# Attention loads reordered with the keys loaded once, and outputs scaled and stored by groups of blocks

## The chip, the cores and the metric

The kernel runs on one core of one Trainium2 chip. The metric is the device time of one execution in microseconds (us). Engines are named as in the profile: PE is TensorE (PEld its weight loads), DVE is VectorE, ACT is ScalarE, POOL is GpSimd, SP is SyncE, which here only issues transfers (DMAs). PEclk is the share of full speed that TensorE's clock was granted.

## What is computed

Two layers of a model over 2048 latent tokens (a grid of 32 rows by 64 columns) behind 256 context tokens, width 1024, all in float32. A layer is: modulation and layer norm, one input projection, three head groups side by side (A: 6 windowed heads on 2 key heads; B: a gated short convolution; C: 6 neighbourhood heads), an output projection, a residual norm, a mixture of 16 experts, a residual norm. The change is in the attention of A and C:

```python
# A: latent queries see a band of +-128 tokens, all context keys and a sink; context queries see the context and the sink
s_win = jnp.einsum('bnqkgd,bnjkd->bnkgqj', qb, kw).astype(jnp.float32) * scale
s_win = jnp.where(valid[None, :, None, None], s_win, NEG_INF)
s_ctx = jnp.einsum('bnqkgd,bjkd->bnkgqj', qb, k_ctx).astype(jnp.float32) * scale
p_win, p_ctx, _ = joint_softmax([s_win, s_ctx, s_sink])
o = (jnp.einsum('bnkgqj,bnjkd->bnqkgd', p_win.astype(v.dtype), vw)
     + jnp.einsum('bnkgqj,bjkd->bnqkgd', p_ctx.astype(v.dtype), v_ctx))
...
# C: a query sees 8 rows x 16 columns around it, with a bias by relative position (rpb), and all context keys
s_nb = s_nb + jnp.transpose(bias, (1, 0, 2, 3, 4))[None].astype(jnp.float32)
s_nb = jnp.where(col_ok[None, None, None, :, None, :], s_nb, NEG_INF)
p_nb, p_ctx = joint_softmax([s_nb, s_ctx])
```

## The kernel before

Every float32 operand of a matmul is split into a high and a low part, and products of parts are added in PSUM. A layer runs four phases one after the other: `phase_in` (projection), `phase_att`, `phase_out` (output projection), `phase_moe`. `phase_in` takes the tokens in five chunks of up to 512; the chunk's transposed input lies in the pool `hT` (two buffers of `hh` and `hl`, taken in turn) and its results (queries QA and QC, keys KA and KC, values VS, the convolution's OB) go to DRAM.

`phase_att` goes through *blocks* in the order of `blist`. A has two units (key heads) of 16 latent blocks and, in layer 0 alone, two context blocks, 36 or 32 blocks of three *members* (the three query heads of 128 tokens). C has six units (heads): in layer 0 a context block (n = 4, two members), and then four blocks (n = 0 to 3) of four members, one per column region. A member passes through `qk` (logits, L1042 and L1043), `soft_max` (bias or mask added, and the minimum, L1064 on DVE), `soft_exp` (L1072 on ACT), transposes on PE, a copy to high parts (L1201 on ACT) and the low parts (L1192 on DVE). When a block's members are through, `pv` multiplies by the values (L1147), copies the sum (L1153, ACT), transposes it (L1160), and then finishes the block: in A the sink's exponent (L1155 DVE, then ACT) and its addition (L1165 DVE); the reciprocal of the sums (L1167 DVE); the addition of high and low halves (L1163 ACT, L1169 DVE); the multiplication by the reciprocal (L1172 DVE); the store, one SP transfer in A (L1174) and for n = 4 (L1176), four in C (L1180; those of the very last block on POOL).

The order on each engine is the order of the program: the loop at L1207 goes through the members three stages apart by the strings ORDERA and ORDERC, and the generators of `pv` advance at "R". Engines wait on one another only by what they read and write.

Transfers. All loads go through SP's queue, in order. At the first member of a block `qk` calls `load_block` up to two blocks ahead (queries, L973 in A and L981 in C; in C also four transfers of the values `vw`, L986) and, at the fifth block of an A unit or the second of a C unit, `load_unit` for the next unit. `load_unit` fetches keys in four transfers of 64 partitions (L948): the high half twice, into partitions 0 to 63 and 64 to 127 of one tile, and the low half twice into another, since queries lie in 128 partitions as [high; low] and the products of both go in one matmul. It also fetches the values (`va` or `vx`) and, by 16 POOL transfers (L962), the table `toep` out of rpb; the very first keys come in two pieces, with maskA (L953) between. `bias_part` (L1004) forms a bias on POOL, three parts for a bias, into one of two buffers (`bias`, and a `va` tile that C no longer needs).

Memory is handed out by pools in order of opening; the first tile of a pool waits for all users of older tiles that lay under the pool. `phase_out` opens its pools over those of attention; the ring of weights (class W) splits raw weights by an ACT cast (L178, called in `_high`) and a DVE subtraction (L186), and its loads of the stored results are L1247 and L1258.

```python
V.tensor_tensor(o[:, :nm, :], o[:, :nm, :], rec["rs"][:, :nm, None].to_broadcast([128, nm, 64]), op=ALU.mult)
```

Of the kernel before, what the change touches and what calls it, by code (L numbers as in the profile page):

```python
# [21 lines left out]
TT = SEQ + CTX  # L22
# [202 lines left out]
def build(ctx, tc, t, out):  # L225
# [279 lines left out]
    def phase_in(l):  # L505
# [5 lines left out]
        hT = {}  # L511
# [102 lines left out]
        def gemm(c):  # L614
# [52 lines left out]
            def b_rest(what, j, pg):  # L667
# [41 lines left out]
                if what == "b":  # L709
# [13 lines left out]
                    for a, o in enumerate((oh, ol)):  # L723
                        for r0, r1, d in runs:
                            (G if c == 4 else SY).dma_start(OB[l][j, :, a, d + r0:d + r1], o.bitcast(F32)[:, r0:r1])
# [169 lines left out]
    def phase_att(l):  # L895
        es = ExitStack()
        kp = es.enter_context(tc.tile_pool(name="at_k", bufs=2))
        qp = es.enter_context(tc.tile_pool(name="at_q", bufs=3))
# [27 lines left out]
        NM = len(mem)  # L926
        ulist = [("A", u) for u in range(2)] + [("C", u) for u in range(6)]
        ustart = {x: min(j for j, b in enumerate(blist) if b[:2] == x) for x in ulist}

        def load_unit(kind, u):  # L930
            r = units[kind, u] = {}
            src = (KA if kind == "A" else KC)[l][u]
            ks = r["k"] = [kp.tile([128, TT], F32R, name=f"k{a}") for a in range(2)]
            vs = VS[l].rearrange("(i p) h d -> p i h d", p=128)
            if kind == "A":
                r["v"] = v = vp.tile([128, NT, 128], F32R, name="va")

            pieces = ((0, 5), (5, NT)) if not blks else ((0, NT),)
            first = not blks
            if first:  # L940
                load_block(blist[0])
            for t0, t1 in pieces:
                if first and t0:
                    for b in blist[1:3]:
                        load_block(b)
                for a in range(2):
                    for b in range(2):
                        SY.dma_start(ks[a].bitcast(F32)[64 * b:64 * b + 64, 128 * t0:128 * t1],  # L948
                                     src[a][:, 128 * t0:128 * t1])
                if t0 == 0 and len(pieces) > 1:  # L950
                    SY.dma_start(maskA, t["maskA"])
                if kind == "A":
                    SY.dma_start(v.bitcast(F32)[:, t0:t1], vs[:, t0:t1, u, :])  # L953
            if kind == "C":
# [3 lines left out]
                tz = bp.tile([128, 16, 48], F32, name="toep", bufs=2)  # L958
# [1006 lines left out]
```

## Time and profile before

| what | value |
|---|---|
| median of 3 runs | 4175.27 us (4169.72 to 4181.32) |
| the profiled execution's own time | 4169.93 us |
| its span | 4168.1 us, 64121 instructions |
| PE, PEld busy | 3816.9 us (92%), 3252.6 us (78%) |
| DVE, ACT, POOL busy | 2906.3 us (70%), 2007.4 us (48%), 826.0 us (20%) |
| transfers | 789.93 MB, mean 190 GB/s |
| attention of layer 0 | about 624 to 1070 us |
| attention of layer 1 | about 2734 to 3170 us |

The span is what the hardware profiler records of one execution. The two attentions are a fifth of it (446 and 436 us). Busy shares over the whole span mix stages with different limits, so the rows below are taken from stretches.

### The profile page before, as it was taken

How to read it: one execution, taken by the hardware profiler on the slowest of the kernel's cores; microseconds unless marked ns; L12 is line 12 of the kernel's file. 1: busy time of each engine (PE TensorE's matmuls, PEld its weight loads, DVE VectorE, ACT ScalarE, POOL GpSimd, SP SyncE). 2: the span in 40 equal slices, each digit the busy share in tenths (PEclk: the TensorE clock that was granted, in tenths of full speed). 3: DMA queues.
4: the chain of work that ended last, by engine and by line, in shares of the span. 5: the costliest groups of instructions: out<-in, count | busy, mean ns of one | idle time of the engine just before them, and what ended most of it. 6: DMA issues, size and time to landing. Idle time of an engine off the chain costs nothing. (4 is left out here: it accounts for less than half of the span.)

```text
span 4168.1 us, 64121 instructions
## 1 busy us (share of the span) xinstructions
PE 3816.9 (92%) x22980; PEld 3252.6 (78%) x22980; DVE 2906.3 (70%) x5836; ACT 2007.4 (48%) x3918; POOL 826.0 (20%) x850
## 2 busy tenths in 40 slices
PE   7999998999998899999997999989989975999983
PEld 5877777888787388989876888778887864999972
DVE  6555557999677477777747765479886776777765
ACT  4344337988433044444424433368775332444453
POOL 0000000144132023323311000011441220222214
PEclk9999998999998999999998999999999986999996
DMA  7566665388643777777766766663786433888885
GB/s 228 170 215 189 203 179 136 82 183 175 226 158 120 217 238 222 211 212 216 210 180 221 220 196 184 174 161 80 147 166 216 168 125 124 251 253 249 246 243 183
DMA packets 733942, 789.93 MB, mean 190 GB/s; under 512 B 121808, under 2 KB 612952, under 8 KB 729784
## 3 DMA queue, kind: packets, MB, share of 16 engines
q1 hardware_dynamic: 692392, 656.83, 54.1%
q0 software_dynamic: 41232, 129.01, 11.4%
q8 instruction: 182, 2.98, 0.3%
q14 instruction: 136, 1.11, 0.1%
HBM read 607.08 MB, written 178.48 MB: 188 GB/s over the span
## 5 line engine op out<-in xcount | busy, mean ns | idle before, releaser
L178 ACT CAST wh<-wraw 128x1024 fp32r<-128x1024 f32 x636 | 656.4, 1049 | 380.8 <-DMA wraw<-in_w_in 132.2
L186 DVE TENSOR_TENSOR wl<-wraw,wh 128x1024 fp32r<-128x1024 f32 x636 | 751.1, 1215 | 17.6 <-ACT wh L178 17.4
L1192 DVE TENSOR_TENSOR pl<-pt,ph 128x256 fp32r<-128x256 f32 (+2 forms) x792 | 359.9, 494 | 21.3 <-ACT ph L1201 16.8
L1201 ACT CAST ph<-pt 128x256 fp32r<-128x256 f32 (+2 forms) x792 | 309.1, 446 | 96.2 <-PE pt L1089 88.7
L626 PE MATMUL gem<-hh,wh 128*128 128x512 f32 (+1 forms) x960 | 355.1, 370 | 0.0
L627 PE MATMUL gem<-hl,wh 128*128 128x512 f32 (+1 forms) x960 | 353.1, 368 | 0.0
L1072 ACT ACTIVATE p<-lg,mx 128x640 f32<-128x640 f32 (+3 forms) x408 | 331.9, 813 | 40.1 <-DVE mx L1064 38.8
L628 PE MATMUL gem<-hh,wl 128*128 128x512 f32 (+1 forms) x960 | 350.6, 365 | 0.0
L1809 PE MATMUL pu<-xh,wh 128*128 128x288 f32 (+1 forms) x1024 | 304.1, 297 | 7.0 <-DVE sa L1637 7.0
L1809 PE MATMUL pa<-xh,wh 128*128 128x288 f32 (+1 forms) x1024 | 300.5, 293 | 0.7 <-DVE modc L419 0.7
L1811 PE MATMUL pa<-xh,wl 128*128 128x288 f32 (+1 forms) x1024 | 296.7, 290 | 0.8 <-DVE wl L186 0.8
L1811 PE MATMUL pu<-xh,wl 128*128 128x288 f32 (+1 forms) x1024 | 296.2, 289 | 0.0
L1810 PE MATMUL pa<-xl,wh 128*128 128x288 f32 (+1 forms) x1024 | 294.0, 287 | 0.0
L1810 PE MATMUL pu<-xl,wh 128*128 128x288 f32 (+1 forms) x1024 | 293.8, 287 | 0.0
L1548 POOL DMA_INDIRECT xe<-H,ix x80 | 161.7, 2021 | 476.3 <-DVE ix L1543 398.3
L1671 POOL DMA_INDIRECT ACC<-y,ix x62 | 128.8, 2077 | 579.6 <-DVE y L1652 326.9
L1846 PE MATMUL py<-wh,gh 128*128 128x512 f32 x512 | 206.4, 403 | 19.6 <-ACT gh L1639 10.8
L804 PE MATMUL gem<-wh,hh 128*128 128x512 f32 x544 | 221.0, 406 | 0.4 <-ACT hh L595 0.4
L805 PE MATMUL gem<-wl,hh 128*128 128x512 f32 x544 | 217.4, 400 | 1.4 <-DVE wl L186 1.4
L806 PE MATMUL gem<-wh,hl 128*128 128x512 f32 x544 | 217.3, 399 | 0.0
L626 PEld LDWEIGHTS gem<-hh,wh 128*128 128x128 f32 x960 | 182.7, 190 | 31.4
L628 PEld LDWEIGHTS gem<-hh,wl 128*128 128x128 f32 x960 | 182.7, 190 | 31.1
(352 smaller groups left out, 9975.1 us busy)
## 6 DMA issues: line engine op xcount, KB each, us to landing
wraw<-in_w_in SPq DMA_DIRECT2D x160, 512.0 KB
wraw<-in_w_gate SPq DMA_DIRECT2D x128, 512.0 KB
wraw<-in_w_up SPq DMA_DIRECT2D x128, 512.0 KB
wraw<-in_w_down SPq DMA_DIRECT2D x128, 512.0 KB
wraw<-in_w_mod SPq DMA_DIRECT2D x88, 512.0 KB
k<-KC SPq DMA_DIRECT2D x48, 576.0 KB
vw<-VS SPq DMA_DIRECT2D x192, 128.0 KB
VS<-vs SPq DMA_DIRECT2D x36, 512.0 KB
```

Source lines behind the costliest of these rows:

```text
L178: self.nc.scalar.copy(h, self.raw[i])
L186: self.nc.vector.tensor_tensor(e[1], self.raw[i], e[0].bitcast(F32), op=ALU.subtract)
L626: P.matmul(pg[:, t0:nt], wh[:, cs_], hh[:, k, t0:nt], start=(k == 0), stop=False)
L627: P.matmul(pg[:, t0:nt], wh[:, cs_], hl[:, k, t0:nt], start=False, stop=False)
L628: P.matmul(pg[:, t0:nt], wl[:, cs_], hh[:, k, t0:nt], start=False, stop=(k == KD - 1))
L804: P.matmul(pg, hh[:, k, tk], wh[:, cs_], start=(k == 0), stop=False)
L1072: S.activation(p[:, 0:768 - w0], rec["lg"][:, w0:768], AF.Exp, bias=st[b]["mx"][:, m:m + 1], scale=-1.0, accum_out=st[b]["ss"][:, m:m + 1])
L1192: V.tensor_tensor(view(st[b]["pl"]), src, view(st[b]["ph"].bitcast(F32)), op=ALU.subtract)
L1201: S.copy(view(st[b]["ph"]), src)
L1809: P.matmul(pp[f], wh[:, cs_], xh[:, kk, :], start=(kk == 0), stop=False)
L1810: P.matmul(pp[f], wh[:, cs_], xl[:, kk, :], start=False, stop=False)
L1811: P.matmul(pp[f], wl[:, cs_], xh[:, kk, :], start=False, stop=(kk == KD - 1))
```

## The change

- `hT` starts with a dummy pair of tiles, so that each chunk uses the other buffer than before. The OB stores of chunk 4 go through ACT's queue instead of POOL's.
- The pools of attention are opened in another order: keys, queries, `vw`, bias, maskA, values, and then the others; the output tiles (`at_o`) come near the end, three tiles of 12 members instead of six of four.
- Keys come as one tile [high; low] by one transfer of 128 partitions. Queries lie in four fixed tiles with two halves, [high; high] and [low; 0]; the zeros are written once per layer by POOL. A block's queries come by three transfers of 64 partitions, three blocks ahead; `vw` stays two ahead.
- `toep` comes by one SP transfer, in rows read backwards by `bias_part`.
- Blocks are put in groups (A: four blocks, or the two context blocks; C: two blocks, or one). Minima, sums, reciprocals and outputs of a group lie in one tile each; L1155, L1165, L1167 and L1172 are done once per group, L1172 on POOL (the last block's on DVE), and the group is stored then.

The diff, cut to its core (removed lines stand in the functions above):

```diff
         last = l == DEPTH - 1
-        hT = {}
+        hT = {-1: [hp.tile([128, KD, 512], F32R, name=z) for z in ("hh", "hl")]}
...
-                            (G if c == 4 else SY).dma_start(OB[l][j, :, a, d + r0:d + r1], o.bitcast(F32)[:, r0:r1])
+                            (S if c == 4 else SY).dma_start(OB[l][j, :, a, d + r0:d + r1], o.bitcast(F32)[:, r0:r1])
...
         kp = es.enter_context(tc.tile_pool(name="at_k", bufs=2))
-        qp = es.enter_context(tc.tile_pool(name="at_q", bufs=3))
+        qp = es.enter_context(tc.tile_pool(name="at_q", bufs=1))
+        vwp = es.enter_context(tc.tile_pool(name="at_vw", bufs=3))
+        bsp = es.enter_context(tc.tile_pool(name="at_bias", bufs=1))
+        mp = es.enter_context(tc.tile_pool(name="at_m", bufs=1))
+        vp = es.enter_context(tc.tile_pool(name="at_v", bufs=2))
         sm = es.enter_context(tc.tile_pool(name="at_s", bufs=4))
         pp = es.enter_context(tc.tile_pool(name="at_p", bufs=3))
         hp = es.enter_context(tc.tile_pool(name="at_h", bufs=2))
-        op = es.enter_context(tc.tile_pool(name="at_o", bufs=6))
         wp = es.enter_context(tc.tile_pool(name="at_w", bufs=2))
-        vp = es.enter_context(tc.tile_pool(name="at_v", bufs=2))
+        op = es.enter_context(tc.tile_pool(name="at_o", bufs=3))
...
-        maskA = bp.tile([128, 640 + 512], F32, name="maskA")
+        maskA = mp.tile([128, 640 + 512], F32, name="maskA")
         maskC = bp.tile([128, 3 * MWID], F32, name="maskC")
-        biases = [None, bp.tile([128, BWID], F32, name="bias")]
+        biases = [None, bsp.tile([128, BWID], F32, name="bias")]
...
+        group = {}
+        for kind, u in [("A", 0), ("A", 1)] + [("C", u) for u in range(6)]:
+            for rows in (range(2, 6), range(6, 10), range(10, 14), range(14, NT), (0, 1)) if kind == "A" else (
+                    ((4,), (0, 1), (2,), (3,)) if u == 5 else ((4,), (0, 1), (2, 3))):
+                for j, n in enumerate(rows):
+                    group[kind, u, n] = ((kind, u, rows[0]), j, len(rows))
...
+        qs = [qp.tile([128, 2, 4, 128], F32R, name=f"q{i}") for i in range(4)]
+        for q in qs:
+            G.memset(q.bitcast(F32)[64:128, 1], 0.0)
...
-            src = (KA if kind == "A" else KC)[l][u]
-            ks = r["k"] = [kp.tile([128, TT], F32R, name=f"k{a}") for a in range(2)]
+            src = (KA if kind == "A" else KC)[l][u].rearrange("a d n -> (a d) n")
+            k = r["k"] = kp.tile([128, TT], F32R, name="k")
             vs = VS[l].rearrange("(i p) h d -> p i h d", p=128)
+            first = loaded[0] == 0
             if kind == "A":
...
+            for t0, t1 in ((0, 5), (5, NT)) if first else ((0, NT),):
+                if first:
+                    more_queries(1 if t0 == 0 else 4)
+                SY.dma_start(k.bitcast(F32)[:, 128 * t0:128 * t1], src[:, 128 * t0:128 * t1])
+                if first and t0 == 0:
                     SY.dma_start(maskA, t["maskA"])
...
-                tz = bp.tile([128, 16, 48], F32, name="toep", bufs=2)
+                tz = bp.tile([128, 16, 64], F32, name="toep", bufs=2)
                 rp = t["rpb"][l, u]
-                tv = tz.rearrange("(a b) i j -> a b i j", a=8)
-                for b in range(16):
-                    G.dma_start(tv[:, b], bass.AP(tensor=rp.tensor, offset=rp.offset + 15 * 64 + 15 - b,
-                                                   ap=[[64, 8], [-64, 16], [1, 48]]))
+                n = 15 * 64 + 48
+                SY.dma_start(tz.rearrange("p i j -> p (i j)")[:, 0:n],
+                             bass.AP(tensor=rp.tensor, offset=rp.offset + 15, ap=[[64, 8], [-1, 16], [1, n]]))
                 r["toep"] = tz
...
+            q = r["q"] = qs[at % 4]
+            for x, a, y in ((0, 0, 0), (0, 1, 0), (1, 0, 1)):
+                dst = q.bitcast(F32)[64 * a:64 * a + 64, x]
+                if kind == "A":
+                    SY.dma_start(dst[:, 0:3], QA[l][3 * u:3 * u + 3, y, :, 128 * n:128 * n + 128].rearrange("m d n -> d m n"))
+                    continue
+                src = QC[l][u][y]
+                if n == 4:
+                    SY.dma_start(dst[:, 0:2], src[:, 0:256].rearrange("p (m q) -> p m q", m=2))
+                else:
+                    SY.dma_start(dst.rearrange("p m (h q) -> p (m h) q", h=2),
+                                 src[:, 256:].rearrange("p (m g q) -> p m g q", m=8, g=4)[:, :, n, :])
...
+            blks[b]["vw"] = vw = vwp.tile([128, 8, 128], F32R, name="vw")
             vsr = VS[l][256:TT, 2 + u, :].rearrange("(r a c) d -> a c r d", a=4, c=64)
             for a in range(4):
                 SY.dma_start(vw.bitcast(F32)[32 * a:32 * a + 32], vsr[a, CG0[n]:CG0[n] + 32])
...
-                            tz[:, i0:i0 + n, j0:j0 + 32], op=ALU.subtract)
-        loaded = [0]
+                            bass.AP(tensor=tz.tensor, offset=tz[:, 15 - i0:16 - i0, j0:j0 + 32].offset,
+                                    ap=[tz.ap[0], [-64, n], [1, 32]]), op=ALU.subtract)
...
                 x = ulist.index((kind, u)) + 1
-                while loaded[0] < min(at + 3, len(blist)):
-                    load_block(blist[loaded[0]])
-                    loaded[0] += 1
+                more_queries(at + 4)
+                more_values(at + 3)
                 if at == ustart[kind, u] + (4 if kind == "A" else 1) and x < len(ulist):
                     load_unit(*ulist[x])
...
-            kh, kl = units[kind, u]["k"]
-            q = blks[b]["q"][:, m, :]
+            k = units[kind, u]["k"]
+            q = blks[b]["q"]
...
-            for x, k in enumerate((kh, kl)):
+            for x in range(2):
                 if win:
-                    P.matmul(pl[:, w0:512], q, win(k), start=(x == 0), stop=(x == 1))
-                P.matmul(pl[:, 512:768], q, k[:, 0:256], start=(x == 0), stop=(x == 1))
+                    P.matmul(pl[:, w0:512], q[:, x, m, :], win(k), start=(x == 0), stop=(x == 1))
+                P.matmul(pl[:, 512:768], q[:, x, m, :], k[:, 0:256], start=(x == 0), stop=(x == 1))
...
             if m == 0:
-                st[b] = {z: sm.tile([128, 4], F32, name=z) for z in ("mx", "ss", "rs")}
+                g, j, ng = group[b]
+                if j == 0:
+                    st["of", g] = {z: sm.tile([128, 12], F32, name=z)[:, 0:ng * nm] for z in ("mx", "ss", "rs")}
+                st[b] = {z: x[:, j * nm:j * nm + nm] for z, x in st["of", g].items()}
...
+            g, j, ng = group[b]
+            of = st["of", g]
+            end = j == ng - 1
+            if end and kind == "A":
+                V.tensor_tensor(of["rs"].rearrange("p (b m) -> p b m", b=ng),
+                                sink[:, None, 3 * u:3 * u + 3].to_broadcast([128, ng, 3]),
+                                of["mx"].rearrange("p (b m) -> p b m", b=ng), op=ALU.subtract)
+                S.activation(of["rs"], of["rs"], AF.Exp, scale=-1.0)
...
-            o = op.tile([128, 4, 64], F32, name="o")
-            S.copy(o[:, :nm, :], px[:, :nm, 64:128])
+            if j == 0:
+                of["o"] = op.tile([128, 12, 64], F32, name="o")[:, 0:ng * nm, :]
+            all_ = of["o"]
+            o = all_[:, j * nm:j * nm + nm, :]
+            S.copy(o, px[:, :nm, 64:128])
+            if end and kind == "A":
+                V.tensor_tensor(of["ss"], of["ss"], of["rs"], op=ALU.add)
+            yield
+            if end:
+                V.reciprocal(of["rs"], of["ss"])
+            yield
+            V.tensor_tensor(o, px[:, :nm, 0:64], o, op=ALU.add)
+            del st[b], blks[b]
+            if not end:
+                return
+            yield
+            yield
+            (V if b == blist[-1] else G).tensor_tensor(all_, all_, of["rs"][:, :, None].to_broadcast([128, ng * nm, 64]),
+                                                       op=ALU.mult)
+            n0 = g[2]
             if kind == "A":
-                V.tensor_tensor(rec["ss"][:, :nm], rec["ss"][:, :nm], rec["rs"][:, :nm], op=ALU.add)
...
-            if kind == "A":
-                SY.dma_start(MIXA[l][128 * n:128 * n + 128, 192 * u:192 * u + 192], o[:, 0:3, :].rearrange("p m d -> p (m d)"))
+                SY.dma_start(MIXA[l][128 * n0:128 * (n0 + ng), 192 * u:192 * u + 192].rearrange("(b p) c -> p b c", p=128),
+                             all_.rearrange("p (b m) d -> p b (m d)", b=ng))
...
+                for x in range(ng):
+                    for m in range(4):
+                        (G if b == blist[-1] else SY).dma_start(dst[m, n0 + x], all_[:, 4 * x + m, :])
+            del st["of", g]
```

## Rows read from the trace of the kernel before

**Rows 1.** Windows: stretch, length; busy us per engine (instructions); PEclk; DMA share; GB/s.

```profile
690.00:840.00 150.00, 147.02 (x1028) 132.30 (x1026) 147.70 (x465) 136.00 (x409) 16.54 (x25) 1.00 0.34 92
842.00:1066.00 224.00, 213.26 (x1548) 188.35 (x1548) 208.82 (x508) 188.82 (x478) 90.16 (x112) 1.00 0.83 176
2932.00:3164.00 232.00, 209.73 (x1479) 189.80 (x1477) 198.66 (x463) 178.30 (x438) 90.28 (x112) 0.95 0.76 161
```

**Rows 2.** Timeline of DVE, one A block: start, duration, instruction.

```profile
781.00 0.86 DVE L1064 CUSTOM_DVE_ANT_0 lg<-lg,maskA,sinks 128x640 f32<-128x640 f32 x1
...
783.65 0.35 DVE L1172 TENSOR_TENSOR o<-o,rs 128x192 f32<-128x192 f32 x1
783.92 0.15 DVE L1155 TENSOR_TENSOR rs<-sinks,mx 128x3 f32<-128x3 f32 x1
784.00 0.88 DVE L1192 TENSOR_TENSOR pl<-pt,ph 128x384 fp32r<-128x384 f32 x2
...
785.60 0.15 DVE L1165 TENSOR_TENSOR ss<-ss,rs 128x3 f32<-128x3 f32 x1
785.78 0.89 DVE L1192 TENSOR_TENSOR pl<-pt,ph 128x384 fp32r<-128x384 f32 x2
786.59 0.17 DVE L1167 RECIPROCAL rs<-ss 128x3 f32<-128x3 f32 x1
786.67 0.86 DVE L1064 CUSTOM_DVE_ANT_0 lg<-lg,maskA,sinks 128x640 f32<-128x640 f32 x1
```

**Rows 3.** First softmax of each layer on DVE (idle before), and SP’s wait.

```profile
631.64 0.76 DVE L1064 CUSTOM_DVE_ANT_0 lg<-lg,maskA,sinks 128x512 f32<-128x512 f32 x1 [10.09 <-PE lg L1043]
...
2740.90 0.76 DVE L1064 CUSTOM_DVE_ANT_0 lg<-lg,maskA,sinks 128x512 f32<-128x512 f32 x1 [9.84 <-DMA maskA<-in_maskA]
...
SPq L973 <- PE gem L628: 8.5, 1, 8.5
```

**Rows 4.** Windows, L1064 alone on DVE: length, busy (records), PEclk, DMA share, GB/s.

```profile
631.60:690.00 58.40, 22.96 (x50) 0.85 0.68 146
2740.90:2795.00 54.10, 22.96 (x50) 0.90 0.75 158
```

**Rows 5.** Waits of PE from 620 to 840: total us, times, longest.

```profile
PE lg L1042 <- DMA k<-KA: 13.0, 3, 4.5
```

**Rows 6.** Windows, C of layer 1: blocks 1 and 2; then 3 and 0.

```profile
2980.95:2997.50 16.55, 16.55 (x124) 15.06 (x124) 16.20 (x39) 14.64 (x37) 3.23 (x4) 1.00 0.62 144
2997.50:3020.45 22.95, 19.25 (x126) 17.65 (x125) 16.65 (x39) 14.96 (x37) 16.02 (x23) 0.85 0.98 184
```

**Rows 7.** Waits of PE from 2700 to 3200.

```profile
PE lg L1042 <- DMA qc<-QC: 17.4, 4, 4.8
```

**Rows 8.** Timeline of SP’s queue, one unit of C in layer 1.

```profile
2950.82 2.38 SPq L948 DMA_DIRECT2D k<-KC  x4
...
2954.39 0.43 SPq L981 DMA_DIRECT2D qc<-QC  x1
```

**Rows 9.** Windows: key loads of 64 partitions; then weights of 128 partitions.

```profile
2993.50:2999.50 6.00, 6.00 (x48) 5.66 (x47) 5.91 (x14) 5.09 (x12) 3.29 (x3) 1.00 1.03 222
3182.00:3198.00 16.00, 15.29 (x68) 11.88 (x67) 5.24 (x8) 2.95 (x5) 0.00 (x0) 1.00 0.92 332
```

**Rows 10.** Groups of DVE, 2932 to 3164: busy, mean ns of one, idle before.

```profile
L1172 DVE TENSOR_TENSOR o<-o,rs 128x256 f32<-128x256 f32 x22 | 20.8, 943 | 0.0
```

**Rows 11.** GpSimd’s bias parts: group of C, layer 0; then its queue’s waits (min/median/max ns).

```profile
L1004 POOL TENSOR_TENSOR bias<-maskC,toep 128x512 f32<-128x512 f32 x8 | 10.3, 1283 | 18.1 <-DVE mx L1064 18.1
...
L1004 POOLq EVENT_SEMAPHORE  x96: 17/30/10038, 746.7 to 3134.8; - x96
```

**Rows 12.** End of attention, layer 0: ACT’s first cast; SP’s wait, 1050 to 1080.

```profile
1070.82 1.99 ACT L178 CAST wh<-wraw 128x1024 fp32r<-128x1024 f32 x2
...
SPq L1247 <- DMA MIXC<-o: 2.7, 1, 2.7
```

More of the change, by code (lines that the diff above doesn't have):

```diff
@@ L964, in load_unit, with load_queries @@
+                SY.dma_start(tz.rearrange("p i j -> p (i j)")[:, 0:n],
+                             bass.AP(tensor=rp.tensor, offset=rp.offset + 15, ap=[[64, 8], [-1, 16], [1, n]]))
                 r["toep"] = tz
-        def load_block(b):
+        def load_queries(at):
+            b = blist[at]
             kind, u, n = b
-            if b in blks:
-                return
-            r = blks[b] = {}
-            if kind == "A":
-                r["q"] = qp.tile([128, 3, 128], F32R, name="qa")
-                SY.dma_start(r["q"].bitcast(F32), QA[l][3 * u:3 * u + 3, :, :, 128 * n:128 * n + 128].rearrange(
-                    "m a d n -> (a d) m n"))
-                return
-            r["q"] = q = qp.tile([128, 4, 128], F32R, name="qc")
-            src = QC[l][u].rearrange("a d n -> (a d) n")
-            if n == 4:
-                SY.dma_start(q.bitcast(F32)[:, 0:2], src[:, 0:256].rearrange("p (m q) -> p m q", m=2))
-                return
-            SY.dma_start(q.bitcast(F32).rearrange("p m (h q) -> p (m h) q", h=2),
-                         src[:, 256:].rearrange("p (m g q) -> p m g q", m=8, g=4)[:, :, n, :])
-            r["vw"] = vw = qp.tile([128, 8, 128], F32R, name="vw")
@@ new lines, in load_queries @@
+            r = blks[b] = {}
+            q = r["q"] = qs[at % 4]
[10 more added lines that the diff above has]
+                                 src[:, 256:].rearrange("p (m g q) -> p m g q", m=8, g=4)[:, :, n, :])
@@ L984, in load_block, with load_values @@
+        def load_values(at):
+            b = blist[at]
+            kind, u, n = b
+            if kind == "A" or n == 4:
+                return
+            blks[b]["vw"] = vw = vwp.tile([128, 8, 128], F32R, name="vw")
             vsr = VS[l][256:TT, 2 + u, :].rearrange("(r a c) d -> a c r d", a=4, c=64)
@@ L986, in load_block, with more_queries, more_values @@
                 SY.dma_start(vw.bitcast(F32)[32 * a:32 * a + 32], vsr[a, CG0[n]:CG0[n] + 32])
+        loaded = [0, 0]
+        def more_queries(n):
+            while loaded[0] < min(n, len(blist)):
+                load_queries(loaded[0])
+                loaded[0] += 1
+        def more_values(n):
+            while loaded[1] < min(n, len(blist)):
+                load_values(loaded[1])
+                loaded[1] += 1
         def bias_part(u, ct, rt):
@@ L1177, in pv @@
             else:
                 dst = MIXC[l][256:TT, 64 * u:64 * u + 64].rearrange("(m a g b) d -> m g a b d", m=4, a=8, g=4)
-                for m in range(4):
-                    (G if b == blist[-1] else SY).dma_start(dst[m, n], o[:, m, :])
-            del st[b], blks[b]
+                for x in range(ng):
+                    for m in range(4):
+                        (G if b == blist[-1] else SY).dma_start(dst[m, n0 + x], all_[:, 4 * x + m, :])
+            del st["of", g]
         gens = []
```

22 lines of the change are left out of this document (1 added, 21 removed).

## The prediction

> **What bounds the kernel now.** The change touches only the two attention stages (about 624 to 1070 us and 2734 to 3170 us of the span), so I read those and leave out the mixture-of-experts and projection stages. First I read the busy time of every engine by stage [rows 1]. In the windowed part (A, 690 to 840 us) VectorE (DVE) works 147.7 of 150 us, TensorE (PE) 147.0, its weight loads 132.3 and ScalarE (ACT) 136.0. In the neighbourhood part (C) of layer 0 PE works 213.3 and DVE 208.8 of 224. In that of layer 1 they work 209.7 and 198.7 of 232: there something outside the engines holds them.
>
> Then I read the order on DVE inside A [rows 2]. From one block's softmax at 781.00 to the next block's at 786.67 are 5.67 us, and each instruction starts when the one before lets go, with no wait noted: DVE has the last word in a steady A block. Of those 5.67 us, start to start, L1172 takes 0.27, L1155 0.08, L1165 0.18 and L1167 0.08.
>
> Then I read what ends the long idle times. Before the first softmax of each layer DVE has idled 10.09 and 9.84 us, and SP, which issues the first loads, has sat 8.5 us waiting for the last projection matmul [rows 3]. The next 58.40 and 54.10 us hold 50 records of L1064 each [rows 4]; a member leaves two, so that is 25 members, or 8.33 blocks, 47.3 us at 5.67. So 11.1 us are lost in layer 0 and 6.8 in layer 1, and PE's waits name the keys there, 13.0 us up to 840 [rows 5]. In C of layer 1, blocks 1 and 2 of a unit take 16.55 us with PE busy all of it, and block 3 with block 0 of the next unit takes 22.95, at a granted clock of 0.85 [rows 6]. The same eight members, 6.4 us more; PE's wait that ends last there is for the queries, 17.4 us in four waits [rows 7]. Those queries left SP at 2954.39, behind the four key transfers of 2950.82 [rows 8].
>
> **The profiled run and the median.** All that follows is subtracted from the profiled execution, 4169.93 us (span 4168.1). The median of the runs is 4175.27, so 5.3 us go back on at the end.
>
> **Part 1, the dummy hT tiles and the new order of pools.** A pool's first tile waits for everybody who used the memory under the pool. Now the queries' pool lies over chunk 4's projection input, whence the 8.5 us. By the sizes in the code, chunk 4 after the change uses the other buffer; keys, queries and maskA then lie over memory that chunk 3 had, and SP can issue them while the last chunk still multiplies. The values' pool (at_v) still reaches into chunk 4's buffer, so `va`, and the second key piece behind it in SP's queue, still wait; but the first softmax needs neither. It could then follow the last matmul as soon as PE is free. I take 10.0 us in layer 0 and 9.8 in layer 1, all of the idle time. Bounds: 0, if one tile of those still overlaps, and 10.1. The OB stores of chunk 4 move from GpSimd's queue to ACT's; ACT works on nothing between the last chunk and the first softmax that SP's loads wait for, so I cost them at nothing; if one did hold ACT's queue, it would delay the first exponentials by its issue time, under 1 us (an SP issue in [rows 8] takes 0.43).
>
> **Part 2, keys once and queries one block earlier.** The four 64-partition key transfers of a unit (2.36 MB, each half twice) become one of 128 partitions (1.18 MB), and three query transfers (1.5 times the bytes) replace one. The number of matmuls stays: the second product runs against a zeroed lower half, which four memsets of GpSimd fill once per layer while the last projection matmuls run (nothing else is in its queue then, so I cost them at nothing). In A the late pieces come earlier, since half the bytes lie ahead of them: I take 10 of the 11.1 us in layer 0 and 6 of the 6.8 in layer 1 (bounds 3 and 11.1; 2 and 6.8; the low ends are what remains if only the bytes matter and `va` still lies in the way). In C of layer 1 the next unit's first queries are now issued ahead of the keys and a block (about 8 us) earlier, more than the longest wait for them, 4.8 us [rows 7]. Five such passages at 6.4 us are 32 us. What is late next is the transfer itself: in the 22.95 us the DMA engines are busy 0.98 of the time and move only 184 GB/s [rows 6]. By bytes, a unit saves 1.18 MB of keys and pays 0.125 MB more for each of four query blocks, 0.5 MB; at the 222 GB/s that the key loads reach [rows 9] that is 5.3 us less and 2.3 us more transfer, net 3.0 of a unit's 39.5 us (16.55 + 22.95). The price of the small runs is not shown, so the net lies between −1 (the query bytes at a third of that rate: 6.8 us for them) and +5. Order and lead are worth more than the sum of bytes; I take 27 of the 32 (bounds 8 and 36, the upper with what part 3 adds).
>
> [...]
>
> **Part 3, the output multiply and the sums once per group.** In A, DVE loses L1172 (0.27) and three quarters of L1155, L1165 and L1167 (0.75 × 0.34 = 0.26): 0.53 of 5.67 us. But the next engine is near: weight loads need 132.3/150 × 5.67 = 5.00, ACT 5.14 (less a little, as one small exponential in four is left), and PE, if its busy time were all work, 5.56. I take 0.35 us per block, between 0.11 (PE's share) and 0.53; it is nearer the upper end because the pipelined matmuls stretch when DVE holds them up, while weight loads don't. 36 blocks make 12.6 us, 32 blocks 11.2. In C the multiply is dear, 943 ns for the 22 of the large form [rows 10], against the 0.27 in A: GpSimd is at work then. That is 20.8 of DVE's 199 us. With DVE relieved PE is the limit: 224 − 213.3 leaves 10.7 us in layer 0; I take 8 (bounds 3 and 16; the upper is the 22 us that the multiplies take less the part that already overlaps). In layer 1 it is inside the 27.
>
> GpSimd takes 48 multiplies of up to 128x768. Its two-input instruction of 128x512 takes 1.28 us [rows 11], so 1.9 us each as an estimate; 48 × 1.9 = 91 us, half per layer, beside 90 us that GpSimd now works in a C stage of 224 [rows 1]. GpSimd has room. The new wait is on SP: the store waits for the multiply, which stands in GpSimd's queue behind bias parts, and these have waited up to 10.04 us for DVE's last softmax on the old bias [rows 11]. Behind the store on SP are the next queries, values and keys; they have three blocks of lead (15 us in A, 24 us in C), so I cost it at nothing. Without that cover it is rival 4. The stores themselves carry the same bytes, in A one transfer for four, in C eight in a burst; SP issues no more of them, so I take 0. The `toep` table in one SP transfer for 16 of GpSimd's per unit saves GpSimd's issues; 0 to 3 us, taken as 0 beyond what C already counts.
>
> **Part 4, the end.** The output tiles (at_o) come to lie under the ring of weights of the output projection. ACT's first cast there, now at 1070.82 [rows 12], must then wait for the last stores to land; the wait for those stores on SP now lasts 2.7 us [rows 12]. Three us per layer is my estimate (bounds 0 and 5).
>
> **Sum.** Layer 0: 10.0 + 10 + 12.6 + 8 − 3 = 37.6. Layer 1: 9.8 + 6 + 11.2 + 27 − 3 = 51.0. Together 88.6; 4169.9 − 88.6 = 4081.3, and with 5.3 for the median 4086.6, say 4086.
>
> **The rivals.**
> 1. PE takes over at once. For it: PE busy 147.0 of 150, and 16.55 of 16.55 in [rows 6]. Against: weight loads have a tenth free, and PE's ends are modelled. A gives 0.11 × 68 = 7.5 instead of 23.8 and C of layer 0 gives 3: 21 less, 4108.
> 2. C of layer 1 stays bound by transfers. For it: busy share 0.98 at 184 GB/s, more bytes of queries in short runs. Against: 0.62 to 0.76 over the rest. Gain 8 instead of 27: 4105.
> 3. The first loads still wait for the last matmul, because one pool still overlaps. The starts give nothing: 4106.
> 4. The other side: SP held up at each group's store, because the multiply is late on GpSimd. The price is 48 groups. To lose the 88.6 and 12.5 more, each needs 2.1 us of real standstill of PE, so the store must block SP 2.1 us beyond the lead of 15 to 24 us. The longest wait of a bias part is 10.04, its own time 1.3 and the multiply's 1.9: 13 us. It decides from there; 4188 or more.
> 5. The keys' layout or the later end cost the gain and other terms fail together: 4163 to 4188.
>
> **How the numbers follow.** Chances: forecast 0.53, rival 1 0.13, rival 2 0.15, rival 3 0.09, rival 4 0.05, rival 5 0.05. Two of the first three rivals together give 4125 to 4130. The low end takes the upper bounds in C (36 and 16, 17 us more), the full 0.53 in A (12 us), no cost at the end (6): 35 less, 4051. I take 4051 to 4130. About 0.3% (12.5 us) is what a measurement of this kernel can tell from no change: faster means under 4162.7, which the forecast, rivals 1 to 3 and their pairs all are: 0.90. Slower is rival 4, 0.05; within 0.05.
>
> **What would show it.** Right: SP's query issues before the last projection matmul; the DVE idle time before the first softmax near zero; L1064 blocks of about 5.3 us in A; no wait for queries at the unit borders of layer 1's C and a granted clock of 1.00 there; the first cast of the output projection about 3 us later. Wrong: an idle time of 10 us before the first softmax (part 1); blocks of 5.5 us or more (rival 1); passages over 20 us at a DMA share near 1 (rival 2); SP waiting over 15 us for GpSimd's multiply with PE waiting behind (rival 4). The prediction also falls if a load that I left alone, `va` or the values of C, becomes the last to land.

## The result, and the profile after

| | before | after |
|---|---|---|
| median, us | 4172.50 (4 runs beside it) | 4124.26 (4120.23 to 4133.57) |
| span of the profiled execution, us | 4168.1 | 4118.7 |

The ratio is 0.9889, with an interval of 0.9873 to 0.9905: 48 us off by the medians, 49.4 by the two profiled spans. The forecast was 89 off, 4086. So the sign held and the time lies in the range, but only a little over half of the expected gain came. Line numbers moved: L1064 is now L1094, L1172 is L1214, L1004 is L1033, the query loads are L984 (A) and L990 (C), the keys L959, `toep` L972, the output stores of C L1226.

The first table is made from the starts of the first softmax of each block on DVE in the two traces (A: first softmax of A to that of C; C: to the last softmax; start: from the last projection matmul to the first softmax; end: from the last softmax to the first matmul of the output projection, L1298 before and L1344 after).

| stage | before, L0 / L1 | after, L0 / L1 | gained | forecast |
|---|---|---|---|---|
| start | 11.7 / 11.5 | 9.7 / 10.5 | 2.0 + 0.9 | 10.0 + 9.8 |
| A | 208.3 / 190.8 | 192.8 / 179.9 | 15.5 + 10.9 | 22.6 + 17.2 |
| C | 222.1 / 229.1 | 216.2 / 209.6 | 5.9 + 19.5 | 8 + 27 |
| end | 15.4 / 15.7 | 18.4 / 18.8 | −3.0 − 3.1 | −3 − 3 |

These add to 48.6 us; the remaining 0.8 lies outside the two attentions. The time outside differs by up to 11 us between the profiled executions of the kernels below (3261.8 us in e9, 3273.0 in e10), so a difference of a few us is read from the stages and not from the whole.

Busy time by stretch of the kernel after (columns as in [rows 1]): eight steady A blocks, C of layer 0, C of layer 1.

```profile
757.05:802.43 45.38, 45.38 (x321) 41.99 (x320) 43.70 (x111) 40.97 (x117) 2.95 (x2) 1.00 0.25 71
...
821.00:1040.00 219.00, 213.51 (x1554) 189.28 (x1553) 193.21 (x471) 190.04 (x483) 70.80 (x70) 1.00 0.77 174
...
2897.00:3110.00 213.00, 205.27 (x1482) 185.40 (x1480) 183.85 (x424) 177.48 (x437) 63.81 (x60) 0.98 0.75 165
```

DVE's work fell as planned, from 208.8 to 193.2 us in C of layer 0, but eight A blocks take 45.38 us, 5.67 each, as before, and PE is busy in all of it. The first softmax of each layer on DVE's timeline, and SP's wait between 600 and 640, which answer to [rows 3]:

```profile
628.63 0.76 DVE L1094 CUSTOM_DVE_ANT_0 lg<-lg,maskA,sinks 128x512 f32<-128x512 f32 x1 [8.09 <-DMA maskA<-in_maskA]
...
2717.04 0.76 DVE L1094 CUSTOM_DVE_ANT_0 lg<-lg,maskA,sinks 128x512 f32<-128x512 f32 x1 [8.90 <-DMA maskA<-in_maskA]
```

```profile
SPq L984 <- PE gem L629: 7.9, 1, 7.9
```

The idle time shrank by 1 to 2 us only, and SP still waits 7.9 us for the last projection matmul. What did change is the stretch behind it (L1094 alone, as in [rows 4]):

```profile
628.60:672.40 43.80, 22.05 (x48) 0.91 0.63 168
...
2717.00:2762.00 45.00, 22.05 (x48) 0.91 0.58 161
```

Eight blocks in 43.8 and 45.0 us, where 8.33 blocks took 58.4 and 54.1: the waits for keys and queries are gone there. In C of layer 1 (waits of POOL and DVE, 2890 to 3110) there is a new one:

```profile
POOL bias L1033 <- DMA toep<-in_rpb: 54.9, 3, 20.5
...
DVE lg L1094 <- POOL bias L1033: 9.8, 3, 5.4
```

and the timelines of SP's queue and of POOL around the worst of them:

```profile
2976.31 5.34 SPq L1226 DMA_DIRECT2D MIXC<-o  x8
...
2985.85 0.45 SPq L959 DMA_DIRECT2D k<-KC  x1
...
2986.82 0.66 SPq L972 DMA_DIRECT2D toep<-in_rpb  x1
```

```profile
3000.02 3.17 POOL L1033 TENSOR_TENSOR bias<-maskC,toep 128x384 f32<-128x384 f32 x3 [20.54 <-DMA toep<-in_rpb]
```

SP issues `toep` at 2986.82, though the block that asks for it began its softmax at 2970.91. SP hardly waits there (its longest wait between 2945 and 3000 is 0.4 us): it issues stores, queries and values one behind the other. `toep` lands 13 us after its issue, and the bias that DVE needs for the next unit is late. The end, against [rows 12]: the first cast came 16.0 us after the last softmax (1037.62), before 8.8 (1070.82 after 1061.99), while the first matmul of the output projection came only 3.0 us later.

```profile
1053.64 1.99 ACT L178 CAST wh<-wraw 128x1024 fp32r<-128x1024 f32 x2 [7.18 <-DMA ml<-OB]
```

### The profile page after: what moved, and what is told of

The parts are those of the page before. It is cut to its first block, busy times and chain, and to the rows that moved or that the text cites. A ratio compares the mean times of both kernels' runs of the same rounds, so it can differ in the third digit from the quotient of the medians.

```text
span 4118.7 us, 63865 instructions
## 1 busy us (share of the span) xinstructions
PE 3803.8 (92%) x22980; PEld 3244.7 (79%) x22980; DVE 2855.8 (69%) x5544; ACT 1999.0 (49%) x3868; POOL 758.8 (18%) x706
## 3 DMA queue, kind: packets, MB, share of 16 engines
q10 hardware_dynamic: 1152, 1.05, 0.1%
## 5 line engine op out<-in xcount | busy, mean ns | idle before, releaser
L1069 PE MATMUL lg<-k,q 128*128 128x384 f32 (+2 forms) x768 | 281.6, 389 | 23.0 <-DMA va<-VS 7.8
L1070 PE MATMUL lg<-k,q 128*128 128x256 f32 x816 | 228.4, 286 | 0.3 <-DVE pl L1238 0.3
L1892 PE MATMUL py<-wh,gh 128*128 128x512 f32 x512 | 206.8, 404 | 17.5 <-ACT gh L1685 11.4
```

Of the source, the lines that this page charges most:

```text
L1069: P.matmul(pl[:, w0:512], q[:, x, m, :], win(k), start=(x == 0), stop=(x == 1))
```

## Experiments

**What bounds a steady A block.** Three kernels. In e2 and e3 one product of `qk` is left out in A (in e2 low queries with the context keys, in e3 all queries with the low context keys); in e4 the outputs are stored unscaled.

```diff
 e2 and e3
-                P.matmul(pl[:, 512:768], ..., start=(x == 0), stop=(x == 1))
+                if kind == "C" or x == 0:
+                    P.matmul(pl[:, 512:768], ..., start=(x == 0), stop=(x == 1 or kind == "A"))
 e4
-            V.tensor_tensor(o[:, :nm, :], o[:, :nm, :], rec["rs"][...], op=ALU.mult)
```

e2, the changed kernel with less for PE:

> The changed kernel without one part of TensorE's work in A: the product of the low query half with the high context keys is left out there (three matmuls of 256 columns per block, about 0.115 us each from start to start, 0.35 us per block). Nothing else of any engine changes. Theory: in steady A blocks TensorE is the bound, which is why the period stayed 5.67 us when DVE lost 0.5 us of it; then the period falls to about 5.33 us, 20 to 24 us less over 68 blocks. Rival: the period is set by a chain of waits through ACT and the two logit buffers, or by DVE still; then it stays 5.67 and under 5 us come off.

e3, the kernel before with less for PE:

> The kernel before with the same matmuls of A left out (low and high query parts times the low context keys, three of 256 columns per block). DVE had 5.67 us of work per block there, by its own row of starts. Theory: DVE and TensorE were both at 5.67 us; with 0.35 us less for TensorE, DVE holds the period, so it stays at 5.6 to 5.67 us and under 6 us come off the kernel before. Rival: only TensorE was the bound and DVE's row of starts was following it; then the period falls to about 5.35 us and 20 to 24 us come off.

e4, the kernel before with less for DVE:

> The kernel before without the multiplication of the outputs by the reciprocal sums (L1172), in A and C: the outputs are stored unscaled, DVE has 122 instructions less. Theory (TensorE is the bound in A): the A blocks stay at 5.67 us; in C, where this multiplication takes up to 1 us beside GpSimd, blocks shorten by 0.1 to 0.3 us, so 3 to 10 us come off in all, nearly all in C. Rival (DVE was the bound, as the prediction had it): A blocks fall by 0.27 us to 5.40, 18 us in A and about 10 in C.

Eight steady blocks (A, second unit, layer 0) as windows; first the kernel before, then e2, e3 and e4:

```profile
775.29:820.69 45.40, 45.40 (x322) 41.78 (x321) 45.12 (x138) 41.58 (x122) 0.00 (x0) 1.00 0.21 60
```

```profile
755.80:799.49 43.69, 43.27 (x299) 38.48 (x298) 42.84 (x111) 41.23 (x117) 2.95 (x2) 1.00 0.26 74
```

```profile
772.98:817.29 44.31, 43.18 (x298) 38.60 (x297) 44.31 (x138) 42.58 (x121) 0.00 (x0) 1.00 0.21 58
```

```profile
774.94:820.37 45.43, 45.43 (x322) 42.02 (x321) 43.74 (x130) 41.57 (x122) 0.00 (x0) 1.00 0.21 60
```

Per block: before 5.68, without DVE's multiplication (e4) 5.68, with less for PE 5.54 in the kernel before (e3) and 5.46 in the changed one (e2). PE is the bound of both kernels at 5.67. DVE stands close behind: when PE gets less in the kernel before, DVE is busy 44.31 of 44.31 and holds the block at 5.54, a little under the theory's 5.60, and the rival (5.35) fell. In the changed kernel DVE no longer holds, but PE's 0.35 us less gave only 0.21: at 5.46 no engine is busy all of the time (PE 43.27 of 43.69, DVE 42.84), and what holds it there stays open. By the medians e2 is 14 us under the changed kernel (20 to 24 were expected); its A stages fell by 6.5 and 7.7 us, while C of layer 0, which e2 leaves as it is, took 224.2 us instead of 216.2, 7 of them in its last unit, where PE waited 4.1 us for queries. So C of layer 0 can lose 7 us at a single border with nothing changed there, and a difference of that size in this stage proves little by itself. Of the other two, e3 is equal to the kernel before (0.9997, 0.9988 to 1.0007; the A stages fell by 3.2 and 0.4 us) and e4 stands at 0.9962 (0.9949 to 0.9975). Of e4's 17 us the attention shows 4.7 in C of layer 0, 1.3 in C of layer 1 and nothing in steady A; the unscaled outputs also go on into the experts' routing, so the rest says nothing of this change.

**Where the multiplication is done.**

```diff
-            (V if b == blist[-1] else G).tensor_tensor(all_, all_, of["rs"]..., op=ALU.mult)
+            V.tensor_tensor(all_, all_, of["rs"]..., op=ALU.mult)
```

> The changed kernel with the group's multiplication on DVE instead of GpSimd (still one per group). Theory: in A nothing moves (TensorE is the bound at 5.67 us and DVE would need about 5.35); in C the multiplication beside GpSimd's bias parts costs DVE 1 to 3 us per group again, against blocks with about 0.3 us of slack, so C gives back 2 to 5 us per layer: 3 to 10 us slower than the changed kernel. Rival: GpSimd's multiplication brought nothing (or its waits on SP cost as much as it saves); then the time is within 3 us, or faster.

12 us slower than the changed kernel by the medians (4136.26), a little over the theory; the attention shows 9 of them. A is 3.8 and 2.8 us longer, which the theory had excluded, C of layer 0 7.2 longer, C of layer 1 3.2 shorter. The loss in C of layer 0 is no single border: its four middle units take 38.0 us each, where they take 36.8 or 36.9 with the multiplication on GpSimd. DVE's groups in C of layer 0 (830 to 1060) and the eight steady A blocks:

```profile
L1214 DVE TENSOR_TENSOR o<-o,rs 128x512 f32<-128x512 f32 x11 | 10.6, 967 | 0.0
```

```profile
762.45:809.21 46.76, 45.47 (x321) 41.88 (x320) 45.46 (x113) 41.37 (x117) 6.34 (x6) 1.00 0.25 69
```

In A it is not the sum that costs (DVE works 45.46 of 46.76, PE 45.47) but the lump: a group of four blocks took 23.38 us instead of 22.69, and one block of the four grew from 5.44 to 5.88.

**The starts.** First the two buffers of hT in pools of their own:

```diff
-        hp = es.enter_context(tc.tile_pool(name="hT", bufs=2))
+        hps = [es.enter_context(tc.tile_pool(name=f"hT{i}", bufs=1)) for i in range(2)]
...
-            hT[c] = [hp.tile([128, KD, 512], F32R, name=z) for z in ("hh", "hl")]
+            hT[c] = [hps[1 - c % 2].tile([128, KD, 512], F32R, name=z) for z in ("hh", "hl")]
```

> The changed kernel with the two buffers of hT in two pools of their own (chunks 1 and 3 in the lower, 0, 2 and 4 in the upper) instead of the dummy tiles, and maskA's pool moved up behind the queries'. Theory: the first query load still waits for the last projection matmul because the wait goes by the whole old pool hT, which the queries' pool touches, and not by the buffer; then it now leaves SP about 8 us earlier, right behind the last KC stores, the keys land near the end of the last projection matmul, and the idle time of DVE before the first softmax falls from about 8.4 and 8.9 us to 1 to 3 us in both layers: 11 to 15 us off the whole. Rival: the first keys are late because the transfers are slow to land (7 us after SP's issue in the changed kernel) and share the engines with the OB and KC stores; then the issue moves but the landing hardly does, and under 5 us come off.

The issue moved as the theory had it (SP's timeline), the first softmax came at 622.46 and 2710.21, 6.2 and 6.8 us earlier, and then the first exponential stood still (ACT's timeline):

```profile
612.10 2.58 SPq L984 DMA_DIRECT2D q<-QA  x3
```

```profile
626.71 1.28 ACT L1102 ACT_TABLE_LOAD   x1 [4.77 <-DMA q<-QA]
```

The first block took 9.56 us instead of 4.87. The ratio to before is 0.9869 (0.9852 to 0.9885), 4 us under the changed kernel by the medians, the spans equal (4118.4): neither theory nor rival. The starts gained 8.0 and 8.2 us, A gave back 4.3 and 2.7 of them and C 3.0 and 3.4. The profile puts the exponential's wait down to a query load; in the program, its tile lies over the convolution's buffers, whose last OB stores leave at 622 to 623. So e9 moves the pools of the softmax, of ph and pl and of the outputs ahead of `vw`, bias and values, and puts the second key piece first:

```diff
         qp = es.enter_context(tc.tile_pool(name="at_q", bufs=1))
-        vwp = es.enter_context(tc.tile_pool(name="at_vw", bufs=3))
-        bsp = es.enter_context(tc.tile_pool(name="at_bias", bufs=1))
...
-        vp = es.enter_context(tc.tile_pool(name="at_v", bufs=2))
...
         op = es.enter_context(tc.tile_pool(name="at_o", bufs=3))
+        vwp = es.enter_context(tc.tile_pool(name="at_vw", bufs=3))
+        bsp = es.enter_context(tc.tile_pool(name="at_bias", bufs=1))
+        vp = es.enter_context(tc.tile_pool(name="at_v", bufs=2))
...
+                if first and t0 == 0:
+                    SY.dma_start(maskA, t["maskA"])
+                    more_queries(2)
+            for t0, t1 in pieces:
+                if kind == "A":
+                    SY.dma_start(v.bitcast(F32)[:, t0:t1], vs[:, t0:t1, u, :])
+                if first and t0 == 0:
+                    more_queries(4)
```

> As e1 (the two buffers of hT in pools of their own), and further: the pools of the softmax (at_s, at_p), of ph and pl (at_h, at_w) and of the outputs (at_o) are moved ahead of vw, bias and the values, and the second key piece is issued ahead of all values and of the third and fourth block's queries. Theory: in e1 the first exponential waited 4.8 us because its tile lay over the convolution's buffers, whose last OB stores had still to leave; with that out of the way the start in both layers comes 5 to 8 us earlier, and at_o no longer lies under the weight ring, which takes the 3 us back at the end of both attentions: 14 to 22 us under the changed kernel in all. Rival: the transfers at the start are crowded, and what the first softmax gains the second key piece or the values lose; then the starts give under 3 us each and only the ends' 6 us remain.

24 us under the changed kernel (4099.95; 0.9838 to before, 0.9822 to 0.9854). From the last projection matmul to the second block's softmax the kernel before takes 18.1 and 17.7 us, the changed one 14.6 and 16.7, e9 7.9 and 7.6: 6.7 and 9.1 us less than the changed one, as the theory had it. C of layer 0 lost 5.2 us in this run, nearly all in its last unit, which e12 below does not show. The end is back at 15.4 us in both layers; the first cast, 8.8 us behind the last softmax (1037.28):

```profile
1046.03 1.99 ACT L178 CAST wh<-wraw 128x1024 fp32r<-128x1024 f32 x2
```

**Keys, queries and their lead.**

```diff
 e7
-                more_queries(at + 4)
+                more_queries(at + 3)
 e10
+                for _ in range(2):
                     SY.dma_start(k.bitcast(F32)[:, 128 * t0:128 * t1], src[:, 128 * t0:128 * t1])
```

> The changed kernel with the queries loaded only two blocks ahead, as before, so that the next unit's first queries go out behind its keys. Theory: lead and order gave most of the 19.5 us that C of layer 1 lost; then 8 to 16 us of them come back as waits for queries at the unit borders, and A loses 0 to 3 us. Rival: the halved key bytes gave it; then the time stays within 4 us.

> The changed kernel with each key transfer issued twice, into the same tile: 1.18 MB more per unit, as many key bytes as before, one more issue on SP per unit. Theory: bytes matter only where the transfers are crowded, the unit borders of C in layer 1 and the second key piece at the start of A: 5 us of transfer more per unit, of which half shows at five borders, 6 to 15 us slower in all. Rival: order and lead alone carried the gain; then under 4 us slower.

e7 is 10 us slower than the changed kernel (4134.75), but not where it was expected: C of layer 0 lost 10.4 us, over its last four units, with six waits of PE for queries (6.5 us), C of layer 1 3.9, A nothing. The queries of A's first blocks, which `load_unit` asks for, go out in e7 as in the change. e10 is 85 us slower (4208.92, 1.0082 to before, 1.0062 to 1.0102): the theory's sign, six times its size. C went to 254.9 and 239.5 us, A to 198.4 and 181.5. PE's waits in C of layer 0 (820 to 1090), and SP's there:

```profile
PE lg L1070 <- DMA q<-QC: 19.3, 4, 5.8
...
SPq L960 <- DMA k<-KC: 35.2, 5, 7.6
```

The second line says that e10 is no test of the bytes alone. Its two key transfers write the same tile, and SP holds the second back until the first has landed: 35.2 us in C of layer 0 and 30.6 in C of layer 1, where these stages lost 38.7 and 30.0 us. Queries and `toep` stand behind the held transfer. The kernel before had no such wait between its four key transfers ([rows 8], four in 2.38 us). So what the key bytes cost by themselves stays open, and with it how the gains in A and in C of layer 1 divide between fewer bytes, earlier queries and the new order. The packets became more and smaller meanwhile: 68035 for 39.4 MB in 224 us of C in layer 0 before, 78511 for 38.1 MB in 219 us now.

**toep.** Three places for its transfer: behind the keys on SP (the change), ahead of them on SP (e11), on GpSimd's queue as 16 transfers (e6) or as the same one (e13).

```diff
 e6
-                SY.dma_start(tz.rearrange("p i j -> p (i j)")[:, 0:n], bass.AP(..., ap=[[64, 8], [-1, 16], [1, n]]))
+                for b in range(16):
+                    G.dma_start(tv[:, b], bass.AP(..., ap=[[64, 8], [-64, 16], [1, 48]]))
 e13
-                SY.dma_start(tz.rearrange("p i j -> p (i j)")[:, 0:n],
+                G.dma_start(tz.rearrange("p i j -> p (i j)")[:, 0:n],
```

> The changed kernel with toep fetched as before, by 16 transfers through GpSimd's queue. In the changed kernel's layer 1 GpSimd waits up to 20.5 us for toep and DVE up to 5.4 us for the bias at the unit borders. Theory: the one SP transfer of toep, issued behind keys and vx in SP's late queue, is what still stretches those borders; then block 3 with block 0 falls from 23.9 and 21.6 us in the two worst to about 16.5, C of layer 1 from 209.6 to 195 to 200 us, 8 to 14 us less in all. Rival: keys and queries land as late (one wait of PE for keys, 1.1 us, stands there), and GpSimd pays 9.5 us of issues per unit; then under 5 us come off.

> The changed kernel with the one SP transfer of toep issued ahead of the unit's keys instead of behind keys and vx. Theory: its place behind 1.18 MB of keys is what makes it late; it then lands about 5 us earlier, and C of layer 1 falls from 209.6 to 198 to 203 us, 6 to 11 us less in all. Rival: it is late because SP's queue as a whole runs late at that point (keys issued 15 us after the block's start) or because the transfer itself is slow; then the borders stay as they are or the keys become late instead, and under 4 us come off.

> The changed kernel with the one transfer of toep (same rows, same bytes) given to GpSimd's queue instead of SP's. Theory (the queue): on SP's queue toep, keys, values and queries stand in one line, and whichever is second is late; on its own queue toep no longer waits for the keys nor the queries for toep, and C of layer 1 falls from 209.6 to about 197 to 200 us as with the 16 transfers: 9 to 14 us less in all. Rival (the form): one transfer of 128 rows of 4032 bytes is slow by itself or takes the engines from the keys wherever it is issued; then C of layer 1 stays above 204 us and under 6 us come off.

Four whole units of C in layer 1 (C1 to C4) as windows; first the kernel before, then after, e6, e11 and e13:

```profile
2969.57:3129.51 159.94, 142.51 (x995) 129.53 (x994) 133.66 (x304) 118.55 (x288) 72.37 (x92) 0.94 0.81 163
```

```profile
2928.97:3074.29 145.32, 139.29 (x1010) 125.84 (x1008) 122.40 (x280) 119.17 (x291) 46.49 (x46) 0.98 0.80 168
```

```profile
2932.84:3066.07 133.23, 133.23 (x995) 121.42 (x993) 122.84 (x280) 117.36 (x288) 84.55 (x109) 1.00 0.90 172
```

```profile
2940.94:3089.03 148.09, 138.14 (x994) 125.77 (x992) 122.82 (x280) 117.41 (x288) 46.97 (x46) 0.96 0.84 165
```

```profile
2936.84:3070.10 133.26, 133.26 (x994) 121.49 (x993) 122.86 (x280) 117.22 (x288) 49.48 (x49) 1.00 0.90 179
```

On GpSimd's queue, in either form, PE is busy all of the four units and the clock is at full speed: 12 us less than the change, 13 in the whole of C. e6 is 14 us under the changed kernel (4110.22), e13 8 (4116.37; its C of layer 0 lost 5.0 us at one border, where PE waited 3.4 us for queries). e11 is 12 us slower (4136.52): in C of layer 1 `toep` still came late, by up to 15.7 us, and the keys then too (3.4 us once); C of layer 0 lost 11.4 us, with four waits of PE for queries (4.9 us). The queue decides, not the form. What fills SP's queue is the issuing itself: over the four units its transfers take 129.7 of 145.3 us to issue, against 87.1 of 159.9 before, and the queries alone 40.4 us in 47 transfers, against 6.5 in 15. In e13 it is 118.6 of 133.3 us, with PE busy throughout: so full a queue delays what stands last in it, and in the changed kernel that was `toep`. In e13 GpSimd issues the `toep` of C's second unit at 2904.77, 7.4 us before the block that asks for it begins its softmax (2912.20); SP, which takes its instructions in order behind stores and `vw`, comes to the one shown above 16 us after the asking block's softmax. How much of the delay is SP's lateness and how much the line of transfers behind it was not separated; in e13 a `toep` transfer takes 8.1 us from issue to landing (median), the one shown above 13.

**All of it.** e9 with e6's `toep`.

> e9 and e6 together: pools apart, second key piece first, at_o off the weight ring, and toep by 16 transfers of GpSimd's queue again. Theory: the parts add, 14 us in C of layer 1 and what e9 gives, so about 28 to 34 us under the changed kernel, near 4092 us. Rival: both relieve the same shortage of transfer time and less than two thirds of the sum comes.

4087.06 us (4081.70 to 4093.05), ratio to before 0.9804 (0.9789 to 0.9818): 37 us under the changed kernel and faster than both. The stages: A 193.7 and 179.7, C 215.9 and 196.7, so the two parts add.

## Why the prediction was right in sign and half in size

**Part 1, the start (forecast 19.8, measured 2.9): rival 3.** The step that failed is "chunk 4 after the change uses the other buffer". In the built program the dummy tiles, which nobody writes, take no place: chunk 4's `hh` lies at the same address as before, under the queries. And the second half of the step, that keys and queries are free of chunk 4 by their own bytes, is not how the wait goes: with the dummy written to, so that the buffers do swap, the program's first query load still waits for chunk 4's last matmul, because its pool touches the old pool hT (read from the program, not run). With two pools the load went out at once (e1). The price of the idle time was right: in e9, after one more wait of the same kind, the starts take 1.7 and 1.6 us, 10.0 and 9.9 under the kernel before.

**Part 2 in A (forecast 16, measured 26.4 with all of A's gain).** The place was right and the size too small. I took the lost time from the first 25 members alone; the borders of the second units, and the first blocks, which without their waits run at 4.9 to 5.4 us, gave the rest. All of A's gain is such stalls. That half the key bytes are what removed them is not shown: e10 takes 7 us of it back, with SP's wait between its key transfers, and e7 none.

**Part 3 in A (forecast 23.8, measured 0): rival 1, and harder than I drew it.** The step that failed is "DVE has the last word in a steady A block". A row of starts without gaps is what a bound engine shows, and also what one shows that runs just as fast as its supplier: DVE had 5.54 us of work (e3), not 5.67, and PE 5.67. I discounted PE's 147.0 of 150 because its ends are modelled; in a window of whole blocks it was 45.40 of 45.40 against DVE's 45.12, and that window was there to be read. That the matmuls stretch where DVE holds them up, while weight loads don't, is what e3 shows, but it is little: 24 fewer of each in eight blocks (the matmuls 2.76 us at 0.115 from start to start) took 2.22 us off PE's busy time and 3.18 off that of the weight loads. That the weight loads had a tenth free, which I set against this rival, told nothing: they took 41.78 us of the same 45.40. The 150 us that I used had context blocks in it.

**Part 3 in C of layer 0 (forecast 8, measured 5.9)** came about as said. With the multiplication back on DVE 7.2 us are lost (e5, in every unit), so that the stage would have gained nothing: 223.4 us against 222.1 before; e4's 4.7 us without L1172 agree, but are less than this stage varies by itself. That the multiply is dear on DVE where GpSimd works shows in the trace of the kernel before: of the 22 on 128x256 in C of layer 0, the 11 with a bias part on GpSimd beside them took 0.66 to 3.20 us, the other 11 0.40 to 0.42; in layer 1 15 took 1.04 to 2.20 and 7 0.41 to 0.42. GpSimd's multiplication takes 1.47 us for 128x768 and 1.05 for 128x512, not 1.9.

**Part 2 in C of layer 1 (forecast 27, measured 19.5).** The queries' waits [rows 7] are gone, as said. What was mis-costed is `toep` on SP, "0 to 3 us, taken as 0": it costs 13 us there (e6, e13). Rival 4 had SP late too, but for another reason, the wait for GpSimd's multiplication, which the trace does not show (SP's longest wait for GpSimd in C is 0.4 us); SP is late because it issues one transfer after another, and I had costed the three query transfers by their bytes and not by SP's time. With `toep` off that queue the stage gains 32.6 us, the 32 that I had counted in the five passages. Whether order and lead are worth more than bytes, as I estimated, stays open: the shorter lead cost 10 us, 4 of them in this stage (e7), and e10 mixes the bytes with a wait.

**Part 4, the end (forecast −6, measured −6.1),** right in place, and undone in e9, which moves at_o among other pools. The size is in part luck: the first cast came 7.2 and 7.5 us later, more than the bound of 5, and only 3.0 and 3.1 of that reached the first matmul.

With the starts and `toep` mended, the time is 4087 us (e12). That it is the time that was forecast is luck, for it comes by another sum, with nothing from A's steady blocks and more from A's stalls and from C of layer 1 (32 us).

No run here changes the number of partitions that a key or a query load writes without changing the bytes or the number of transfers as well, so the share of that number in these gains and costs was not separated.

## What to carry to other kernels

Where two engines are both nearly full, cut the window to whole periods, and take work from one and then from the other: the one whose cut shortens the period is the bound (here 5.68 to 5.54 us by PE's cut, nothing by DVE's). A load moved to another queue is costed by what stands before it in that queue, the issue times included, and not by its bytes: the same `toep` transfer on GpSimd's queue left the four units of C in layer 1 12 us shorter (e13). A test that doubles a load needs a second tile to write to, or it tests a wait along with the bytes (35.2 us of it in C of layer 0 of e10). And before a start is costed as free, look in the program at what the first load waits for; a freed buffer isn't a freed pool (SP's first wait stayed at 7.9 us, where it had been 8.5).

## What had not been expected of the hardware

Issuing alone can nearly fill a queue. In the four units of C in layer 1 SP's issuing instructions took 129.7 of 145.3 us, while the DMA share was 0.80 (0.81 before). A query transfer took 0.86 us to issue on average, where the one of the kernel before took 0.43. The profile's busy shares leave such instructions out, so only SP's own timeline shows it.
